# Weight chunks into one more place and in their filling order, and the last norm in halves ahead of the branch

## The chip, the cores and the metric

The kernel runs on one core of a Trainium2 chip. Its time is that of one launch in microseconds (us), the median of three runs. Matmuls run on TensorE (PE), element-wise work on VectorE (DVE), ScalarE (ACT) and GpSimd (POOL); SyncE (SP) issues nearly all DMAs, one after the other, from one queue. Where SP stands in a wait, every DMA written behind it waits too.

## The reference

Two blocks run over 256 tokens of width 1024. The first has two layers, each a mixer and 16 experts; the second has a token mixer and 32 experts, and a last norm. What matters here, cut down:

```python
def expert_choice_ffn(h, w_router, w_gate, w_up, w_down):   # 16 experts, 32 tokens each
    aff = softmax(h @ w_router)
    gate, idx = top_k(swapaxes(aff, 1, 2), cap)
    xe = h[bidx, idx]
    a = einsum('becd,edf->becf', xe, w_gate)
    u = einsum('becd,edf->becf', xe, w_up)
    ye = einsum('becf,efd->becd', silu(a) * u, w_down)
    return zeros_like(h).at[bidx, idx].add(gate[..., None] * ye)

def rmsnorm(x, g):
    return x * rsqrt(mean(x * x, axis=-1) + eps) * g
```

Every expert has three float32 matrices of its own, so nearly all bytes that the kernel reads are expert weights.

## The kernel before

**Stages.** `body` runs `mixer` and `experts` for layer 0 and for layer 1, then `token_mixer` and `moe`, then `final`. In each expert stage the weights come as chunks of 128 partitions x 2048 floats (1024 KB): `w_eg` and `w_ed` in the two layers, `w2eg` and `w2ed` in `moe`. PE reads a chunk at L810 (`w_eg`), L863 (`w_ed`), L1485 (`w2eg`) and L1524 (`w2ed`). In the mixers the weights are chunks too; there each is split into a high and a low part (L101, L102) and used at L121 to L123.

**Places.** `K.chunk` puts a chunk into a place of the tag that the ring names next: `K.use("WT")` means one in a W place, one in a T place, and so on in turn. There are 9 W places and 12 T places of 8 KB per partition. T places also hold whole tiles of the mixers (the names in `WHOLE`). Within a tag the places are taken in turn, so a chunk waits until the last reader of the tag's oldest place is done, even when a place of the other tag is free. At the start of an expert stage `ROOM` (or `ROOM2`) lists the tags of the chunks that are fetched ahead, while the mixer and the router still run; later chunks follow the ring set by the next `K.use`.

**Small places.** Tag P is four tiles of 2 KB per partition, taken in turn by softmax tiles, squares, `gs`, `yt`, `mt` and by `gb`, which a DMA fills in `ada_gate` (L632 and L633). Tag PT has four more, with `ht`, `sg` and others; `wh` and `wl` have three each, for the split weights. A DMA into such a tile stands on SP until the reader of the tile's former content is done.

**Order.** A scheduler fixes the order of instructions on each engine when the kernel is built. SP keeps the order in which the fetches are written (`issue_after` at L57).

**The end.** `moe_quad` does four experts together: the gate and up matmuls, then for each half of 512 columns the down matmuls (L1524), the scaling into `yt` (L1527), the split into `yd`, and the addition into `h` (L1533, L1535). Behind the last quad each engine loads a count (L1438) and branches (L1440): a second round, for tokens above the capacity, is skipped. Then `final` takes the squares of `h`, the inverse root (`rs`) and four products, and SP sends each out (L1546).

Of the kernel before, what the change touches and what calls it, by code (L numbers as in the profile page):

```python
# [2 lines left out]

# [1 line left out]

# [27 lines left out]
class Core:  # L33
    def __init__(self, ctx, tc, A):
        self.tc, self.nc, self.A = tc, tc.nc, A
        self.const = ctx.enter_context(tc.tile_pool(name="const", bufs=1))
        self.sb = ctx.enter_context(tc.tile_pool(name="sb", bufs=1))
        self.ps = ctx.enter_context(tc.tile_pool(name="ps", bufs=1, space=PSUM))
        self.flip = self.nsplit = self.nchunk = 0

        self.share = 4
        self.after = nullcontext
        self.idle, self.pre, self.sent = (), [], None
        self.use("W")

    def load(self, name, shape, dt=F):
# [116 lines left out]
    def rstd(self, src, n=D, dve=True, tag="P"):  # L163
        nc = self.nc
        ss = self.t([128, 2, 2], "ss", 2)
        for c in range(2):
            sl = slice(c * 512, (c + 1) * 512)
            for tt in range(2):
                sq = self.t([128, 512], "sq", SMALL[tag], tag=tag)
                if tt and dve:  # L170
# [546 lines left out]
def experts(K, h, l, mix, ada, prep, ahead=None):  # L717
# [74 lines left out]

    K.use(ROOM)
    ws = [K.chunk(A["w_eg"][l, i // KD, i % KD]) for i in range(len(ROOM))]
    K.use("WT" if ahead else FEW)
    hid, Ge = [], []
    gw = K.t([128, 4], "gw4")
    for e in range(NE):
# [19 lines left out]
        gs = K.t([128, 512], "gs", NP, tag="P")  # L818
# [628 lines left out]
def moe_round(K, h, hn, cmb, slot, gate=None):  # L1447
    nc, A = K.nc, K.A
    for q in range(NE2 // 8):
        oh = K.t([128, 2, 8, CAP2], "oh", 2, tag="oa", dt=FR)  # L1450
        for tt in range(2):
            nc.vector.tensor_tensor(oh[:, tt], slot[:, tt, 8 * q:8 * q + 8].unsqueeze(2).to_broadcast([128, 8, CAP2]),
                                    K.iota[:, 1:CAP2 + 1].unsqueeze(1).to_broadcast([128, 8, CAP2]), OP.is_equal)
        xT = K.t([128, KD, T], "xT", tag="hTa")
        for kb in range(KD):
            p = K.bank("sc")
            for n, (part_, tt) in enumerate(((0, 0), (0, 1), (1, 0), (1, 1))):
                nc.tensor.matmul(p[:, :T], lhsT=hn[part_][:, tt, kb * 128:(kb + 1) * 128],
                                 rhs=oh[:, tt].rearrange("p a b -> p (a b)"), start=(n == 0), stop=(n == 3))
            if kb % 2:  # L1460
                nc.scalar.activation(xT[:, kb, :], p[:, :T], AF.Identity, bias=K.B2[:, kb:kb + 1], scale=K.A2[:, kb:kb + 1])
            else:
                nc.vector.tensor_scalar(xT[:, kb, :], p[:, :T], K.A2[:, kb:kb + 1], K.B2[:, kb:kb + 1],
                                        op0=OP.mult, op1=OP.add)
        for i in (0, 4):
            moe_quad(K, h, xT, oh, cmb, 8 * q + i, i, gate)
            gate = None


def moe_quad(K, h, xT, oh, cmb, e, i, gate):  # L1470

    nc, A = K.nc, K.A
    hid = []
# [1 line left out]
    for pr in range(2):  # L1475
# [23 lines left out]
        if pr == 0:  # L1499
# [13 lines left out]
            for x in range(4):  # L1513
                nc.vector.tensor_copy(gw[32 * x:32 * x + 32, :], p[32 * x:32 * x + 32, T + x:T + x + 1])
    yd = K.t([128, 2, 1024], "yd", tag="V", dt=FR)
    for hf in range(2):
        sl = slice(hf * 512, (hf + 1) * 512)
        dn = K.bank("acc")
# [7 lines left out]
        y = K.t([128, 512], "yt", NP, tag="P")  # L1526
        nc.vector.scalar_tensor_tensor(y, dn, gw, K.gt[:, 1, sl], op0=OP.mult, op1=OP.mult)  # L1527
        hi, lo = yd[:, 0, sl], yd[:, 1, sl]
        K.split_to(hi, lo, y)
        for tt in range(2):  # L1530
            p = K.bank("sc")
            for n, part_ in enumerate((hi, lo)):
                nc.tensor.matmul(p, lhsT=Ge[:, tt * 128:(tt + 1) * 128], rhs=part_, start=(n == 0), stop=(n == 1))  # L1533
            hs = h[:, tt, sl]
            nc.vector.tensor_add(hs, p, hs)  # L1535


def final(K, h, out):
    nc = K.nc
    y = K.t([128, 2, D], "y", tag="hn")  # L1540
    rs = K.rstd(h)
    for tt in range(2):
        for c in range(2):
            sl = slice(c * 512, (c + 1) * 512)
            nc.vector.scalar_tensor_tensor(y[:, tt, sl], h[:, tt, sl], rs[:, tt:tt + 1], K.gf[:, sl], op0=OP.mult, op1=OP.mult)
            nc.sync.dma_start(out=out[:, tt, sl], in_=y[:, tt, sl])  # L1546
# [203 lines left out]
```

## Time and profile before

| what | value |
|---|---|
| median of 3 runs | 2229.97 us (2227.25 to 2230.5) |
| profiled execution | 2231.4 us |
| its span in the profile | 2229.6 us |
| mean granted TensorE clock | 0.915 |
| PE busy | 1803.5 us (81%) |
| DVE, ACT, POOL busy | 761.1, 600.3, 222.2 us |
| moved by DMA | 748.83 MB, mean 336 GB/s |
| chain that ended last | PE 40%, DMA 29%, issue 22%, DVE 6%, ACT 2% |

A single launch is profiled; 1.8 us of it lie outside the span. Times in rows count from the start of the span. The page cuts the span into 40 slices of 55.7 us.

### The profile page before, as it was taken

The numbers are of one execution on the slowest core, as the hardware profiler recorded it, in microseconds if no ns is written. First come the engines' busy times: TensorE is split into PE (matmuls) and PEld (weight loads), VectorE is DVE, ScalarE is ACT, GpSimd is POOL, SyncE is SP. The second block draws the span as 40 slices with busy tenths as digits, with TensorE's granted clock in tenths as the row PEclk, the third lists the DMA queues.
The fourth block names the chain that finished last, engine by engine and source line by source line (L and its number), as shares of the span: only waits on it lengthen the run. The fifth ranks groups of instructions, "written<-read, shape, count | busy, mean of one in ns | idle before, by whom it ended". The sixth has DMA issues, their size and how long they took to land.

```text
span 2229.6 us, 30070 instructions
## 1 busy us (share of the span) xinstructions
PE 1803.5 (81%) x12172; PEld 1017.9 (46%) x12172; DVE 761.1 (34%) x1696; ACT 600.3 (27%) x1191; POOL 222.2 (10%) x183
## 2 busy tenths in 40 slices
PE   8999996666699998987788666789999867676765
PEld 8888631110277776841234123368888412121211
DVE  5666510000045588532111111157557311111112
ACT  4666410000033357620125100055245200000000
POOL 2111200000011122300000000033134000000000
PEclk9999997777799999997799778889999999999998
DMA  8445779999999953569999999984223999999996
GB/s 342 149 146 207 313 311 420 422 421 421 421 418 419 414 210 151 216 264 399 420 420 420 421 419 420 418 337 156 76 70 149 418 420 421 420 421 421 421 421 284
DMA packets 108442, 748.83 MB, mean 336 GB/s; under 512 B 14120, under 2 KB 14537, under 8 KB 18697
## 3 DMA queue, kind: packets, MB, share of 16 engines
q1 hardware_dynamic: 107752, 745.79, 82.3%
q8 instruction: 98, 1.61, 0.3%
q10 hardware_dynamic: 544, 1.05, 0.1%
q14 instruction: 48, 0.39, 0.1%
HBM read 745.74 MB, written 1.05 MB: 335 GB/s over the span
## 4 chain that ended last, share of the span: by engine, by line
PE 40%; DMA 29%; issue 22%; DVE 6%; ACT 2%; POOL 0%; POOLq 0%; SPq 0%; ACTq 0%; DVEq 0%
DMA w<-in_w_eg 18%; DMA w<-in_w_ed 9%; PE mm L121 7%; PE mm L122 6%; PE mm L123 6%; PE acc L863 4%; PE mm L810 3%; PE sc L889 2%; DVE wl L102 1%; PE acc L518 1%; DMA w<-in_w2z 1%; PE acc L949 1%; PE acc L1228 1%; DMA cx<-in_ctx 1%; PE sc L122 1%
## 5 line engine op out<-in xcount | busy, mean ns | idle before, releaser
L810 PE MATMUL mm<-w,xT 128*32 128x512 f32 x2048 | 327.8, 743 | 116.6 <-DMA w<-in_w_eg 116.2
L101 ACT ACTIVATE wh<-w 128x512 fp32r<-128x512 f32 x384 | 239.9, 630 | 290.5 <-PE mm L122 218.0
L121 PE MATMUL mm<-hTa,wh 128*128 128x256 f32 x960 | 281.0, 294 | 5.6 <-DVE Ga L245 1.7
L123 PE MATMUL mm<-hTa,wl 128*128 128x256 f32 x960 | 274.2, 288 | 1.9 <-DVE wl L102 1.6
L122 PE MATMUL mm<-hTb,wh 128*128 128x256 f32 x960 | 272.5, 285 | 2.2 <-DVE hTb L113 1.6
L102 DVE TENSOR_TENSOR wl<-w,wh 128x512 fp32r<-128x512 f32 x286 | 220.1, 775 | 108.9 <-ACT wh L101 106.1
L1485 PE MATMUL mm<-w,xT 128*32 128x512 f32 x1024 | 176.9, 613 | 71.9 <-DMA w<-in_w2eg 71.4
L863 PE MATMUL acc<-w,hid 128*32 128x256 f32 x2048 | 184.7, 449 | 62.3 <-DMA w<-in_w_ed 62.3
L102 POOL TENSOR_TENSOR wl<-w,wh 128x512 fp32r<-128x512 f32 x98 | 129.0, 1317 | 901.9 <-ACT wh L101 803.9
L810 PEld LDWEIGHTS mm<-w,xT 128*32 128x32 f32 x2048 | 51.3, 120 | 329.6 <-DMA w<-in_w_eg 271.6
L121 PEld LDWEIGHTS mm<-hTa,wh 128*128 128x128 f32 x960 | 181.8, 190 | 28.4 <-issue 15.7
L123 PEld LDWEIGHTS mm<-hTa,wl 128*128 128x128 f32 x960 | 181.0, 190 | 10.6 <-issue 3.4
L122 PEld LDWEIGHTS mm<-hTb,wh 128*128 128x128 f32 x960 | 182.0, 190 | 6.2 <-issue 2.4
L863 PEld LDWEIGHTS acc<-w,hid 128*32 128x32 f32 x2048 | 80.5, 128 | 148.6 <-DMA w<-in_w_ed 83.1
L1524 PE MATMUL acc<-w,work 128*32 128x512 f32 x512 | 94.9, 640 | 32.9 <-DMA w<-in_w2ed 32.9
L1485 PEld LDWEIGHTS mm<-w,xT 128*32 128x32 f32 x1024 | 34.2, 110 | 189.1 <-DMA w<-in_w2eg 140.8
L178 POOL TENSOR_TENSOR rs<-rs,mhalf 128x2 f32<-128x2 f32 x9 | 6.8, 751 | 1008.4 <-DVE rs L177 1008.4
L826 DVE TENSOR_TENSOR hid<-tp,sg 128x256 f32<-128x256 f32 x32 | 13.6, 425 | 216.8 <-ACT sg L825 216.8
L113 DVE SCALAR_TENSOR_TENSOR yd<-acc,gw,yd 128x256 fp32r<-128x256 f32 x32 | 15.5, 483 | 181.2 <-ACT yd L112 181.2
L112 ACT ACTIVATE yd<-acc,gw 128x256 fp32r<-128x256 f32 x32 | 15.2, 475 | 220.0 <-PE acc L863 220.0
L91 DVE COPY gs<-mm 128x512 f32<-128x512 f32 x16 | 11.1, 692 | 181.5 <-PE mm L810 181.5
L825 ACT ACTIVATE sg<-tp 128x256 f32<-128x256 f32 x32 | 12.3, 384 | 218.3 <-PE tp L822 218.3
(468 smaller groups left out, 2471.8 us busy)
## 6 DMA issues: line engine op xcount, KB each, us to landing
w<-in_w_eg SPq DMA_DIRECT2D x256, 1024.0 KB, 19.8
w<-in_w_ed SPq DMA_DIRECT2D x128, 1024.0 KB, 18.5
w<-in_w2eg SPq DMA_DIRECT2D x128, 1024.0 KB, 19.8
w<-in_w2ed SPq DMA_DIRECT2D x63, 1024.0 KB, 19.8
w<-in_ada SPq DMA_DIRECT2D x24, 1024.0 KB, 11.7
w<-in_w_in SPq DMA_DIRECT2D x22, 1024.0 KB, 7.2
w<-in_wk SPq DMA_DIRECT2D x20, 1024.0 KB, 17.7
w<-in_w_b SPq DMA_DIRECT2D x8, 1024.0 KB, 6.0
```

The lines of the kernel that those rows point to most:

```text
L101: self.hi = nc.scalar.activation(hi, src, AF.Copy)
L102: (nc.gpsimd if n in self.idle or n % self.share == self.share - 1 else nc.vector).tensor_tensor(lo, src, hi.bitcast(F), OP.subtract)
L121: mm(out, lhsT=l[0], rhs=r[0], start=start, stop=False)
L122: mm(out, lhsT=l[0], rhs=r[1], start=False, stop=False)
L123: mm(out, lhsT=l[1], rhs=r[0], start=False, stop=stop)
L518: nc.tensor.matmul(po[half * 64:half * 64 + 64, :T], lhsT=V[:, kt, c:c + 64], rhs=PTs[half][:, kt * 256:(kt + 1) * 256], start=(kt == 0), ...
L810: nc.tensor.matmul(gu[32 * j:32 * j + 32, :], lhsT=xT[:, k, (e % 8) * CAP:(e % 8 + 1) * CAP], rhs=w[:, j * 512:(j + 1) * 512], start=(k == ...
L863: nc.tensor.matmul(dn[32 * x:32 * x + 32, :T], lhsT=hid[e // 8][:, e % 8, f, hh * 32:hh * 32 + 32], rhs=ws[x][:, fb * T:(fb + 1) * T], sta ...
L889: nc.tensor.matmul(p[:, :T], lhsT=hn[:, tt, kb * 128:(kb + 1) * 128], rhs=oh[:, tt].rearrange("p a b -> p (a b)"), start=(tt == 0), stop=( ...
L949: nc.tensor.matmul(p[:, :T], lhsT=w[:, o:o + 128], rhs=cT[:, k, :], start=(k == 0), stop=(k == KD - 1))
L1485: nc.tensor.matmul(gu[o:o + 32, :], lhsT=xT[:, k, y:y + CAP2], rhs=ws[x][:, (2 * kk + j) * 512:(2 * kk + j + 1) * 512], start=(k == 0), st ...
L1524: nc.tensor.matmul(dn[32 * x:32 * x + 32, :], lhsT=hid[x][:, c, :], rhs=wd[x][:, c * 512:(c + 1) * 512], start=(c == 0), stop=(c == 3), ti ...
```

## The change

1. The four P tiles of their own are gone. Tag P now takes a quarter of one T tile, held for a mixer; the room makes a 13th T place.
2. `ROOM` has 21 entries in place of 19 and `ROOM2` 18 in place of 16: one more T, and one "Q", a chunk that is fetched as four pieces of 512 columns into three `wh` tiles and a `wl` tile. The rings behind them (`AGAIN`, `AGAIN2`) repeat the order in which the places were filled.
3. `gb`, `gs` and `yt` move from P to PT.
4. In `moe_quad` the second half's down matmuls are written ahead of the first half's addition.
5. The last norm works in halves: the squares and the product with `gf` of half 0 stand in the last quad, the rest behind it and ahead of the branch; half 0 is scaled and sent by ACT, half 1 by DVE and SP. The same stands once more inside the branch.

```diff
     def chunk(self, src, parts=1):
         tag = next(self.ring)
+        if tag == "Q":
+            return self.quarters(src, ("wh", "wh", "wh", "wl"))
...
     def t(self, shape, name, bufs=1, tag=None, dt=F):
         tag = tag or name
+        if tag == "P":
+            if self.held is None:
+                self.held = self.sb.tile([128, PW], F, name="P4", tag="T", bufs=PLACES["T"]), cycle(range(0, PW, 512))
+            o = next(self.held[1])
+            return self.held[0][:, o:o + shape[1]]
...
-ROOM2 = "TWWTTTTWWTTTWWWW"
-ROOM, FEW = "TWWWWTTTTTTWWTTTWWW", "WWWWTWWWWWT"
-PLACES = {"W": 9, "T": 12}
+AGAIN, AGAIN2 = "WWWWTTTTTTWWTTTWWW", "WWTTTTWWTTTWWWW"
+ROOM2 = "TTWWTTTTWWTTQTWWWW"
+ROOM, FEW = "TTWWWWTTTTTTWWTTQTWWW", "WWWWTWWWWWT"
+PLACES = {"W": 9, "T": 13}
...
-    gb = K.t([128, 512], "gb", NP, tag="P")
+    gb = K.t([128, 512], "gb", NP, tag="PT")
...
-    K.use("WT" if ahead else FEW)
+    K.use(AGAIN if ahead else FEW, AGAIN)
...
     K.pre = [K.chunk(A["w2eg"][2 * i + x, c]) for i in range(2) for c in range(4) for x in range(2)]
-    K.use("WWTWT")
+    K.pre += [K.chunk(A["w2ed"][x, 0]) for x in range(len(ROOM2) - 16)]
+    K.use(AGAIN2)
...
-    moe_round(K, h, hs, cmb, slot, gate)
+    y = Final(K, h, out)
+    moe_round(K, h, hs, cmb, slot, gate, y.first)
+    y.second()
     n = nc.values_load(mi[0:1, 0:1], min_val=0, max_val=T)
...
+        if hf:
+            add(0)
+            if end and early:
+                early()
...
+    def first(self):
+        self.y = self.K.t([128, 2, D], "y", tag="hn")
+        self.squares(0)
+        for tt in range(2):
+            self.K.nc.vector.tensor_mul(self.y[:, tt, :512], self.h[:, tt, :512], self.K.gf[:, :512])
+
+    def second(self):
+        K, nc, y = self.K, self.K.nc, self.y
+        self.squares(1)
+        rs = K.inverse(self.ss)
+        for tt in range(2):
+            nc.scalar.activation(y[:, tt, :512], y[:, tt, :512], AF.Identity, scale=rs[:, tt:tt + 1])
+            nc.scalar.dma_start(out=self.out[:, tt, :512], in_=y[:, tt, :512])
+            nc.vector.scalar_tensor_tensor(y[:, tt, 512:], self.h[:, tt, 512:], rs[:, tt:tt + 1], K.gf[:, 512:], op0=OP.mult, op1=OP.mult)
+            nc.sync.dma_start(out=self.out[:, tt, 512:], in_=y[:, tt, 512:])
```

**SP at the start of the second block** (`token_mixer`): the last fetches of the gate's weights (`in_ada`), then `gb`, then the first weights of the mixer (`in_w2z`). In brackets stand the counters that an issue waits for: DMAHW0 to 7 count landings, the others are engines. Before:

```order
L58 DMA w<-in_ada 128x2048 [waits DMAHW5_49,PE_49]
L58 DMA w<-in_ada 128x2048 [waits DMAHW6_49,PE_49]
L58 DMA gb<-in_gtb 128x512 [waits DMAHW7_49,Activation_49]
L58 DMA w<-in_w2z 128x2048 [waits DMAHW0_49,PE_49]
L58 DMA w<-in_w2z 128x2048 [waits DMAHW1_49,PE_49]
```

And after the change:

```order
L58 DMA w<-in_ada 128x2048 [waits DMAHW3_49,PE_49]
L58 DMA w<-in_ada 128x2048 [waits DMAHW4_49,PE_49]
L58 DMA gb<-in_gtb 128x512 [waits DMAHW5_49,DVE_49,Activation_49]
L58 DMA w<-in_w2z 128x2048 [waits DMAHW6_49,PE_49]
L58 DMA w<-in_w2z 128x2048 [waits DMAHW7_49,PE_49]
```

The order of issues is the same; `gb` now waits for DVE as well. The PT tile that it takes held the fifth of the eight `ht` tiles of this block's start, whose last reader is the fifth `hTb` subtraction on DVE (L1052 before).

**SP at the start of the last expert stage** (`moe`): the gate's weights, `gb`, and the first chunks fetched ahead (`in_w2eg`). Before:

```order
L58 DMA w<-in_ada 128x2048 [waits DMAHW7_49,DVE_49,Pool_49]
L58 DMA gb<-in_gtb 128x512 [waits DMAHW0_49,Activation_49,Pool_49]
L58 DMA w<-in_w2eg 128x2048 [waits DMAHW1_49,PE_49]
L58 DMA w<-in_w2eg 128x2048 [waits DMAHW2_49]
L58 DMA w<-in_w2eg 128x2048 [waits DMAHW3_49]
```

And after the change:

```order
L58 DMA w<-in_ada 128x2048 [waits DMAHW5_49,DVE_49,Pool_49]
L58 DMA gb<-in_gtb 128x512 [waits DMAHW6_49]
L58 DMA w<-in_w2eg 128x2048 [waits DMAHW7_49,PE_49]
L58 DMA w<-in_w2eg 128x2048 [waits DMAHW0_49,PE_49]
L58 DMA w<-in_w2eg 128x2048 [waits DMAHW1_49,DVE_49,Pool_49]
```

Here `gb` no longer waits for ACT and POOL, only for a landing among its own counters; the chunks behind it have waits for engines of their own.

**PE and DVE at the end**, up to the branch: L1519 is the gate and up matmul (L1485 before), L1568 the down matmul (L1524), L1556 the addition's matmul (L1533). PE after the change:

```order
L1519 MATMUL mm<-w,xT 32x512 x32
L1526 MATMUL tp<-ident,work 128x128 x4
L1568 MATMUL acc<-w,work 32x512 x16
L1556 MATMUL sc<-yd,Ge 128x512 x4
L1568 MATMUL acc<-w,work 32x512 x16
L1556 MATMUL sc<-yd,Ge 128x512 x4
L1468 TENSOR_LOAD mi
```

DVE after the change:

```order
L1558 TENSOR_TENSOR h<-sc,h 128x512 x2
L1602 TENSOR_TENSOR y<-h,gf_13339 128x512
L1594 ISA sq,ss<-h 128x512
L1594 ISA ss 128x1
L1602 TENSOR_TENSOR y<-h,gf_13339 128x512
L1575 SCALAR_TENSOR_TENSOR yt<-acc,gw,gt 128x512
L126 TENSOR_TENSOR yd<-yt,yd 128x512
L1558 TENSOR_TENSOR h<-sc,h 128x512 x2
L1594 ISA sq,ss<-h 128x512
L1594 ISA ss 128x1
L197 TENSOR_TENSOR rs<-ss 128x2
L198 TENSOR_SCALAR rs<-rs 128x2
```

PE's order in the last quad is as it was before: 16 down matmuls, 4 of the addition, 16, 4. On DVE two products and a square of half 0 moved ahead of `yt` of half 1, and the rest of the norm ahead of the branch.

## Rows read from the trace of the kernel before

**Rows 1.** The page: GB/s moved in each of 40 slices of 55.7 us.

```profile
GB/s 342 149 146 207 313 311 420 422 421 421 421 418 419 414 210 151 216 264 399 420 420 420 421 419 420 418 337 156 76 70 149 418 420 421 420 421 421 421 421 284
```

**Rows 2.** Windows: busy us (instructions) of PE, PEld, DVE, ACT, POOL; PEclk, DMA share, GB/s.

```profile
280.00:290.00 10.00, 10.00 (x66) 4.57 (x65) 3.06 (x16) 0.95 (x2) 0.00 (x0) 1.00 0.28 107
...
610.00:790.00 180.00, 176.48 (x1636) 133.50 (x1628) 93.93 (x148) 60.42 (x107) 24.74 (x20) 0.99 1.01 415
```

**Rows 3.** Timeline of SP, layer 0's experts: start, us, instruction, count.

```profile
283.23 0.33 SPq L58 DMA_DIRECT2D w<-in_w_eg  x1
...
294.30 0.80 SPq L58 DMA_DIRECT2D w<-in_w_eg  x2
```

**Rows 4.** Timeline of PE at the third chunk read in layer 0's experts.

```profile
284.94 1.06 PE L810 MATMUL mm<-w,xT 128*32 128x512 f32 x8
```

**Rows 5.** DMA issues from 282 to 293 us: count, KB, us to landing.

```profile
w<-in_w_eg SPq DMA_DIRECT2D x1, 1024.0 KB, 4.7
```

**Rows 6.** Timeline of SP, layer 1's experts.

```profile
972.93 0.33 SPq L58 DMA_DIRECT2D w<-in_w_eg  x1
...
974.98 0.33 SPq L58 DMA_DIRECT2D w<-in_w_eg  x1
...
997.67 0.33 SPq L58 DMA_DIRECT2D w<-in_w_eg  x1
...
1002.71 0.33 SPq L58 DMA_DIRECT2D w<-in_w_eg  x1
```

**Rows 7.** Start of the last expert stage: SP's issues and wait, PE's last readers.

```profile
1687.27 0.33 SPq L58 DMA_DIRECT2D w<-in_ada  x1
...
1726.09 0.33 SPq L58 DMA_DIRECT2D gb<-in_gtb  x1
1726.51 15.33 SPq L58 DMA_DIRECT2D w<-in_w2eg  x13
...
SPq L58 <- POOL h L1317: 18.8, 1, 18.8
...
1710.89 0.28 PE L123 MATMUL mm<-yb,wl 128*128 128x256 f32 x1
...
1737.84 0.40 PE L123 MATMUL mm<-wh,mTb 128*128 128x512 f32 x1
```

**Rows 8.** Start of the second block: SP, DVE, PE, and two windows.

```profile
1460.78 0.33 SPq L58 DMA_DIRECT2D gb<-in_gtb  x1
...
1472.64 1.09 DVE L1052 TENSOR_TENSOR hTb<-ht,hTa 128x256 fp32r<-128x256 f32 x3
...
1468.44 0.58 PE L121 MATMUL mm<-hTa,wh 128*128 128x256 f32 x1
...
1470.00:1480.00 10.00, 7.96 (x60) 7.43 (x60) 7.03 (x17) 7.77 (x15) 2.97 (x3) 0.95 1.01 424
1480.00:1490.00 10.00, 10.00 (x87) 10.00 (x86) 3.47 (x5) 6.06 (x13) 6.48 (x6) 1.00 1.01 416
```

**Rows 9.** The end: timeline, the branch on PE, the landing of the outputs.

```profile
2213.10 0.75 DVE L1527 SCALAR_TENSOR_TENSOR yt<-acc,gw,gt 128x512 f32<-128x512 f32 x1 [2.60 <-PE acc L1524]
...
2215.84 1.29 DVE L1535 TENSOR_TENSOR h<-sc,h 128x512 f32<-128x512 f32 x2 [0.59 <-PE sc L1533]
2219.87 0.69 DVE L171 CUSTOM_DVE_ANT_0 sq<-h 128x512 f32<-128x512 f32 x1 [2.75 <-DVEq L1440]
2222.46 2.74 DVE L1545 SCALAR_TENSOR_TENSOR y<-h,rs,gf 128x512 f32<-128x512 f32 x4 [0.81 <-POOL rs L178]
...
L1440 PEldq COMPARE_BRANCH  x1: 3635/3635/3635, 2215.9 to 2215.9; - x1
...
out_y<-y SPq DMA_DIRECT2D x4, 256.0 KB, 3.2
```

**Rows 10.** The instructions that write tiles of tag P: count, ns min/median/max.

```profile
L417 ACT ACTIVATE P<-P,m x80: 492/506/725, 78.4 to 890.6; 128x256 f32<-128x256 f32 x64, 128x512 f32<-128x512 f32 x16
...
L506 DVE TENSOR_SCALAR P<-P,r x64: 341/349/1368, 134.4 to 894.3; 128x256 f32<-128x256 f32 x64
```

More of the change, by code (lines that the diff above doesn't have):

```diff
@@ L1 @@
 from contextlib import ExitStack, nullcontext
-from itertools import cycle, islice
+from itertools import chain, cycle, islice
 import numpy as np
@@ L42, in __init__ @@
         self.after = nullcontext
-        self.idle, self.pre, self.sent = (), [], None
+        self.idle, self.pre, self.sent, self.held = (), [], None, None
         self.use("W")
@@ L49, in load, with use @@
         return t
-    def use(self, places):
-        self.ring = cycle(places)
+    def use(self, places, first=""):
+        self.ring = chain(first, cycle(places))
     def fetch(self, out, src):
@@ L67, in chunk, with quarters @@
         return t
+    def quarters(self, src, tags):
+        ts = []
+        for i, tag in enumerate(tags):
+            ts.append(self.sb.tile([128, 512], F, name="w4", tag=tag, bufs=SMALL[tag]))
+            self.fetch(ts[-1], src[:, i * 512:(i + 1) * 512])
+        return Quarters(ts)
     def next_chunk(self, src, parts=1):
@@ L174, in rstd, with inverse @@
                     nc.scalar.activation(sq, src[:, tt, sl], AF.Square, accum_out=ss[:, tt, c:c + 1])
+        return self.inverse(ss, n)
+    def inverse(self, ss, n=D):
+        nc = self.nc
         r = self.t([128, 2], "rs", 2)
@@ L324, in mixer @@
     nc, A = K.nc, K.A
+    K.held = None
     if ahead:
@@ L724, in experts @@
         next(rt)
+    K.held = None
     q = K.logits
@@ L817, in experts @@
             hid.append(K.t([128, 8, 4, 64], "hid", tag=own[e // 8]))
[L818 removed]
+        gs = K.t([128, 512], "gs", NP, tag="PT")
         K.copy(gs, gu)
@@ L1033, in token_mixer @@
     nc, A, tc = K.nc, K.A, K.tc
+    K.held = None
     sc = K.t([128, 2, D], "sincos", tag="V")
@@ L1326, in token_mixer, with moe @@
         yield
-def moe(K, h, mix):
+def moe(K, h, mix, out):
     nc, A, tc = K.nc, K.A, K.tc
@@ L1344, in moe @@
         next(rt)
+    K.held = None
     q = K.logits
@@ L1444, in moe, with moe_round @@
             moe_round(K, h, hs, cmb, slot)
-def moe_round(K, h, hn, cmb, slot, gate=None):
+        K.sent = None
+        y = Final(K, h, out)
+        y.first()
+        y.second()
+def moe_round(K, h, hn, cmb, slot, gate=None, early=None):
     nc, A = K.nc, K.A
@@ L1465, in moe_round, with moe_quad @@
         for i in (0, 4):
-            moe_quad(K, h, xT, oh, cmb, 8 * q + i, i, gate)
+            moe_quad(K, h, xT, oh, cmb, 8 * q + i, i, gate, early)
             gate = None
-def moe_quad(K, h, xT, oh, cmb, e, i, gate):
+def moe_quad(K, h, xT, oh, cmb, e, i, gate, early):
     nc, A = K.nc, K.A
@@ L1515, in moe_quad, with add @@
     yd = K.t([128, 2, 1024], "yd", tag="V", dt=FR)
+    def add(hf):
+        sl = slice(hf * 512, (hf + 1) * 512)
+        for tt in range(2):
+            p = K.bank("sc")
+            for n, part_ in enumerate((yd[:, 0, sl], yd[:, 1, sl])):
+                nc.tensor.matmul(p, lhsT=Ge[:, tt * 128:(tt + 1) * 128], rhs=part_, start=(n == 0), stop=(n == 1))
+            hs = h[:, tt, sl]
+            nc.vector.tensor_add(hs, p, hs)
     for hf in range(2):
@@ L1525, in moe_quad @@
                                  start=(c == 0), stop=(c == 3), tile_position=(0, 32 * x))
-        y = K.t([128, 512], "yt", NP, tag="P")
-        nc.vector.scalar_tensor_tensor(y, dn, gw, K.gt[:, 1, sl], op0=OP.mult, op1=OP.mult)
-        hi, lo = yd[:, 0, sl], yd[:, 1, sl]
-        K.split_to(hi, lo, y)
-        for tt in range(2):
[L1531 to L1535, printed above, removed]
@@ L1538, in final @@
[L1538 to L1546, printed above, removed]
+        if hf:
+            add(0)
+            if end and early:
+                early()
+        y = K.t([128, 512], "yt", NP, tag="PT")
@@ new lines, in moe_quad, with __init__, squares @@
+        nc.vector.scalar_tensor_tensor(y, dn, gw, K.gt[:, 1, sl], op0=OP.mult, op1=OP.mult)
+        K.split_to(yd[:, 0, sl], yd[:, 1, sl], y)
+    add(1)
+class Final:
+    def __init__(self, K, h, out):
+        self.K, self.h, self.out = K, h, out
+        self.ss = K.t([128, 2, 2], "ss", 2)
+    def squares(self, c):
+        K, nc = self.K, self.K.nc
+        sl = slice(c * 512, (c + 1) * 512)
+        for tt in range(2):
+            sq = K.t([128, 512], "sq", NP, tag="PT")
+            h, ss = self.h[:, tt, sl], self.ss[:, tt, c:c + 1]
+            if tt:
+                nc.vector.tensor_tensor_reduce(sq, h, h, 1.0, 0.0, OP.mult, OP.add, ss)
+            else:
+                nc.scalar.activation(sq, h, AF.Square, accum_out=ss)
+    def first(self):
[7 more added lines that the diff above has]
+        rs = K.inverse(self.ss)
+        for tt in range(2):
+            nc.scalar.activation(y[:, tt, :512], y[:, tt, :512], AF.Identity, scale=rs[:, tt:tt + 1])
+            nc.scalar.dma_start(out=self.out[:, tt, :512], in_=y[:, tt, :512])
+            nc.vector.scalar_tensor_tensor(y[:, tt, 512:], self.h[:, tt, 512:], rs[:, tt:tt + 1], K.gf[:, 512:],
+                                           op0=OP.mult, op1=OP.mult)
+            nc.sync.dma_start(out=self.out[:, tt, 512:], in_=y[:, tt, 512:])
@@ L1576, in body @@
         dbg("h1", h)
-        moe(K, h, token_mixer(K, h))
+        moe(K, h, token_mixer(K, h), out)
         dbg("h3", h)
-        final(K, h, out)
 QORDER = [4 * (2 * (b // 4) + half) + b % 4 for b in range(8) for half in range(2)]
```

## The prediction

> **What bounds the kernel now.** I read the slices of the page first. About 420 GB/s are moved in three long stretches [rows 1], the expert stages: there a chunk of 1024 KB (1.049 MB) takes 1.049 MB / 421 GB/s = 2.49 us, and PE waits for it. Between the stretches the mixers are bound by computing. Where DMA is the bound to the end of a stretch, its length is bytes over rate, so time can be won only at its start: every chunk that lands earlier, before the queue is full for good, shifts all that follows by 2.49 us. I call that the lead. From 610 to 790 us both PE (176.5 of 180 us) and DMA are full [rows 2]; PE there works on what it got late, so a lead passes through.
>
> Next I read the starts of the stretches in the windows and on SP. In layer 0 the DMA share is 0.28 from 280 to 290 us, while PE is at 10.00 of 10 [rows 2]. SP issues one chunk at 283.23 and the next only at 294.30 [rows 3], though PE has finished a chunk every 2.05 us: two issues that wait for consecutive chunks, 972.93 and 974.98, show this pace [rows 6]. The ring asks for a T place there while W places stand free. A chunk issued into an idle queue lands after 4.7 us [rows 5], that is 2.2 us of start and 2.49 of transfer; so DMA is busy from 2.2 us after an issue on.
>
> **The change part by part.** All terms are made against the profiled execution (2231.4 us, span 2229.6); the median lies 1.4 us below it.
>
> *Layer 0's experts.* Two more chunks are fetched ahead (the 13th T place and the quarters). The first issue of the ring then waits for the third chunk read, whose matmuls end at 284.94 + 1.06 = 286.0 [rows 4]; I followed the tags of the new ring through, and its places come free in that order, about 2.05 us apart, which is faster than 2.49. So DMA is full from 286.0 + 2.2 = 288.2. Before, it was full from 294.30 + 2.2 = 296.5, with one chunk moved till then. Lead: 2 + (296.5 - 288.2) / 2.49 - 1 = 4.33 chunks = 10.8 us.
>
> *Layer 1's experts.* Before, seven chunks are issued from 972.93 to 997.67, and the queue fills from 1002.71 + 2.2 = 1004.9 [rows 6]. After, the ring starts with the release of 974.98, so DMA is full from 977.2: 2 + (1004.9 - 977.2) / 2.49 - 7 = 6.1 chunks, 15.3 us. Later in this stage the FEW ring follows, and by my walk through its places one issue is held near 1012 us for a chunk that PE reads late; I take 2 us off for it (a choice; 0 to 4). Lead: 13.2 us.
>
> *The last expert stage.* SP issues the last of `in_ada` at 1687.27 and `gb` only at 1726.09, because the P tile waits for POOL's addition at L1317; the w2eg chunks behind it start at 1726.51 [rows 7]. In PT the order shows `gb` waiting for neither ACT nor POOL, so it goes at about 1687.7. Of the chunks behind it the first finds its place free near 1695, the second when the matmul at 1710.89 ends, 1711.2 [rows 7], and seven more follow by 1728. DMA is full from 1711.2 + 2.2 = 1713.4, before from 1728.7: (1728.7 - 1713.4) / 2.49 + 1 = 7.1 chunks, 17.8 us. The next place comes free only with the matmul that ends at 1738.2 [rows 7], while the nine chunks are in by 1735.8: idle till 1740.2, 4.4 us given back. A second stall, where chunks behind the fetched-ahead ones wait for the first expert matmuls, I set at 2.5 us (0 to 5). Lead: 10.9 us. Nothing after 1730 is bound by PE for long, so this lead reaches the end.
>
> *The end.* Before, `h` is complete at 2215.84 + 1.29 = 2217.13; then DVE and ACT stand until PE's branch of 3.6 us (2215.9 to 2219.5) is over, squares of both halves start at 2219.87, and the products end at 2222.46 + 2.74 = 2225.20 [rows 9]. After, the squares and products of half 0 (0.69 + 0.77 + 0.69 = 2.15 us on DVE) lie in DVE's idle 2.60 us ahead of `yt` [rows 9]; without that cover they cost 2.15. Behind 2217.13 come one square (0.77), the chain from the last square to the first product (2221.18 to 2222.46, 1.28) and two products of 0.69 on DVE, with ACT beside it: 2220.55, 4.65 us earlier. SP now stands for the landing of the outputs (3.2 us) and only then branches. ACT, DVE and PE branch under that landing; for SP's branch I take 0.3 us, between nothing and PE's 3.6. Gain 4.3 us, range 1 to 4.7.
>
> The Trainium skill (Advanced Engine Details and Errata, Control Flow Timing) gives a compare-and-branch about 108 ns. The trace shows 3.6 us for PE's, and the measurement decides; by the page the branch held nothing and the gain here would be 3.5 us less, the sum 30.2.
>
> *Second half ahead of the first's addition.* PE's order in the last quad reads as before, 16, 4, 16, 4; other quads wait for DMA anyway. Nothing.
>
> *`gb` at the start of the second block.* This one costs. Before, it goes at 1460.78 and w2z behind it at once; PE starts on w2z at 1468.44 [rows 8]. Now `gb` waits for the fifth `hTb`, the first of three that start at 1472.64 [rows 8]: 1473.1 at the latest, about 1471.2 without the splits of w2z that lie between them before. Behind `gb` on SP stand all weights of the mixer. w2z is issued at 1471.6, lands with `gb` ahead of it near 1476.9, is split in 0.6 us, and PE starts at 1477.5, 9.1 us late. But before, PE did only 60 matmuls from 1470 to 1480, against 87 per 10 us afterwards [rows 8], because `hTb` came in piece by piece; after, all of it is there. 60 matmuls at 8.7 per us take 6.9 us, so they are done at 1484.4 in place of 1480: 4.4 us. With a slower first piece I take 5.5 us, range 3 to 9.1. PE is at 10.00 from 1480 on, so the delay goes through to the last stage.
>
> *P as quarters of one tile, `gs` and `yt` in PT.* No wait that I can name comes with it; DVE and ACT change their order a little in the mixers. Four operations of 0.75 us, as `yt` [rows 9], bound it from both sides: 0, range -3 to +3.
>
> Sum: 10.8 + 13.2 + 10.9 + 4.3 - 5.5 = 33.7 us. Profiled 2231.4 - 33.7 = 2197.7; the median, 1.4 lower, 2196.
>
> **The rivals.**
> (a) *Places only.* The order of places brings nothing, because the chunks that come free earlier only pile up ahead of a PE that is full (10.00 from 280 to 290 [rows 2]). Then two chunks per layer stage remain: 5.0 + 5.0 + 10.9 + 4.3 - 5.5 = 19.7 us, 2210. Against it: PE's 2.05 us per chunk is faster than 2.49, so it catches up within the stage.
> (b) *No loss at `gb`.* PE catches up after w2z, as DMA has weights waiting when it starts. 39.2 us, 2191.
> (c) *The quarters cost.* Four DMAs of 256 KB for one chunk. An output of 256 KB lands after 3.2 us [rows 9]; one after the other that is 12.8 us in place of 4.7, 8.1 us in each of three stages: 33.7 - 24.3 = 9.4, 2220. Against it: the four are issued back to back into a queue that is otherwise not full, and share it.
> The Trainium skill (DMA: Bandwidth & Descriptors, Rules for kernel authors) asks for at least 1 MiB per DMA, which speaks against the quarters. The outputs' 3.2 us for 256 KB beside 4.7 us for 1024 KB agree in direction; whether pieces that overlap pay it no row here shows.
> (d) *Slower.* The quarters of the held tile act as one place: each new P tile waits for the last read of its neighbours. L417 writes 80 softmax tiles, 506 ns each, and L506 scales 64 of them again, 349 ns [rows 10]. If each of the 80 waits for one such pair, 0.86 us, that is 68 us: 2231.4 + 68 - 33.7, median 2264. From 33.7 / 80 = 0.42 us per tile on it is slower. Against it: the order shows the softmax steps of neighbouring tiles still interleaved.
>
> **How the numbers follow.** Forecast 0.65; (a) 0.12; (b) 0.11; (c) 0.06; (d) 0.06. The forecast's own terms reach from about 2188 to 2206. The range 2187 to 2213 holds the forecast, (a) and (b) and leaves out (c) and (d) and the ends of the others. A difference under 0.2% (4.5 us) can't be told from none. Forecast, (a), (b) and (c) are faster by more than that, with 0.02 for a mixture that ends within it; (d) is slower where its wait per tile passes 0.42 us, 0.05 of its 0.06.
>
> **What would show it.** SP's issues in layer 0's experts at 286.0, 288, 290 and on, DMA full from about 288; in layer 1's from about 977. `gb` of the last stage at about 1688 (shifted by the leads so far) and w2eg right behind it. PE's first L121 of the second block some 9 us later against its layer's end, and the mixer 5 us longer. No idle of ACT and DVE for the branch, and outputs issued 3.5 us behind the last `h`. I am wrong if DMA falls idle again later in a stage by what it gained at the start, if the mixers of the first block grow by more than 3 us, or if a full second block hides a start that is 9 us late.

## The result and the profile after

The changed kernel takes 2201.83 us, median of 4 runs (2201.07 to 2202.3), beside 2229.28 us for the kernel before in the same runs: ratio 0.9877, 95% interval 0.986 to 0.9895. It is 27.5 us faster; 33.7 was forecast, and the time lies in the range. The profiled execution took 2202.3 us, its span is 2200.5 us, 29.1 less than before.

First the page of the changed kernel, GB/s in 40 slices (of 55.0 us now):

```profile
GB/s 342 142 151 229 321 348 420 421 421 421 420 418 420 416 214 154 234 339 396 420 420 420 420 420 420 418 286 170 77 58 264 353 421 420 421 420 420 421 421 298
```

Beside [rows 1] the three stretches at 420 are as high as they were; what rose are the slices ahead of them: 313, 311 became 321, 348; 216, 264 became 234, 339; 70, 149 became 58, 264. The time was won at the starts, not in the stretches.

To see where it was won I set the same instruction of both traces side by side (the n-th matmul of a line, counted from the start). Minus means earlier after the change:

| instruction | before | after | shift |
|---|---|---|---|
| first expert matmul of layer 0 (L810) | 280.04 | 279.37 | -0.7 |
| first w_ed matmul of layer 0 (L863) | 569.86 | 559.45 | -10.4 |
| first expert matmul of layer 1 | 969.74 | 958.47 | -11.3 |
| last expert matmul of layer 1 | 1451.72 | 1427.54 | -24.2 |
| 1345th L121, end of the token mixer | 1723.60 | 1705.61 | -18.0 |
| first expert matmul of the last stage (L1485) | 1756.83 | 1739.99 | -16.8 |
| last expert matmul (L1524) | 2212.39 | 2185.40 | -27.0 |
| end of the span | 2229.6 | 2200.5 | -29.1 |

So layer 0 gave 10.4 (forecast 10.8), layer 1 12.9 (13.2), the start of the second block cost 6.2 (5.5), the last expert stage gave 9.0 (10.9), and the end 2.1 (4.3). The rest, 0.9, lies between the two marks: 0.5 by the last w_ed matmul of layer 0 (781.07 to 770.18), 0.4 in the mixer of layer 1.

These are single executions, and they scatter. The kernels of experiments 1, 2, 7, 8 and 9 run the same instructions as the change up to the end of layer 1; their shifts are -6.3 to -11 at layer 0's first w_ed matmul, -9.8 to -12.9 at layer 1's first expert matmul and -23.7 to -26.6 at its end. So the layers agree with the forecast to within 2 or 3 us; that they agree to 0.4 is luck.

**The starts of the layers.** Windows of the kernel before, where DMA idled (columns as in [rows 2]; layer 0, then layer 1):

```profile
290.00:300.00 10.00, 10.00 (x65) 4.05 (x62) 1.79 (x4) 2.51 (x4) 0.00 (x0) 1.00 0.49 177
...
990.00:1000.00 10.00, 10.00 (x68) 4.42 (x66) 1.45 (x3) 1.37 (x3) 0.00 (x0) 1.00 0.32 117
```

Windows of the changed kernel, where layer 1 runs 11.3 us earlier, and SP's first issues behind the chunks fetched ahead:

```profile
280.00:290.00 10.00, 10.00 (x64) 4.96 (x60) 2.56 (x13) 0.95 (x2) 0.00 (x0) 1.00 0.36 130
290.00:300.00 10.00, 10.00 (x63) 4.08 (x62) 2.00 (x4) 2.51 (x4) 0.00 (x0) 1.00 0.95 382
...
980.00:990.00 10.00, 10.00 (x71) 3.90 (x70) 1.67 (x4) 0.95 (x2) 0.00 (x0) 1.00 1.01 420
```

```profile
285.39 0.33 SPq L58 DMA_DIRECT2D w<-in_w_eg  x1
287.45 0.33 SPq L58 DMA_DIRECT2D w<-in_w_eg  x1
...
963.71 0.33 SPq L58 DMA_DIRECT2D w<-in_w_eg  x1
965.77 0.33 SPq L58 DMA_DIRECT2D w<-in_w_eg  x1
```

In place of one issue and a gap of 11 us [rows 3] stand issues 2.06 us apart, from 285.39 (286.0 was forecast, less the 0.7 of the first row of the table); in layer 1 from 963.71, which is 974.98 less 11.3, as forecast. DMA is at 0.95 and 1.01 where it was at 0.49 and 0.32 before.

**The two gb tiles.** SP and PE of the changed kernel, at the start of the second block and of the last expert stage:

```profile
1446.30 0.33 SPq L58 DMA_DIRECT2D gb<-in_gtb  x1
...
1452.88 0.58 PE L137 MATMUL mm<-hTa,wh 128*128 128x256 f32 x1 [7.61 <-ACT wh L117]
...
1669.76 0.44 SPq L58 DMA_DIRECT2D gb<-in_gtb  x1
1677.15 0.33 SPq L58 DMA_DIRECT2D w<-in_w2eg  x1
...
1693.21 0.80 SPq L58 DMA_DIRECT2D w<-in_w2eg  x2
...
1720.01 1.28 SPq L58 DMA_DIRECT2D w<-in_w2eg  x3
```

On the old time scale (24.2 us later) the first `gb` goes at 1470.5 where it went at 1460.78 [rows 8], and PE stands 7.61 us until w2z is there and split. The second goes at 1669.76; in the last stage (18.0 us later on the old scale) the chunks follow at 1695.1, 1711.2 and 1738.0, the three times that the prediction took from [rows 7].

**The end.** Timeline of the changed kernel from the last addition into `h`:

```profile
2188.76 1.29 DVE L1558 TENSOR_TENSOR h<-sc,h 128x512 f32<-128x512 f32 x2 [0.59 <-PE sc L1556]
...
2190.08 0.69 DVE L1594 CUSTOM_DVE_ANT_0 sq<-h 128x512 f32<-128x512 f32 x1
...
2192.06 1.33 ACT L1609 ACTIVATE y<-y,rs 128x512 f32<-128x512 f32 x2 [1.79 <-POOL rs L199]
2192.06 1.41 DVE L1611 SCALAR_TENSOR_TENSOR y<-h,rs,gf 128x512 f32<-128x512 f32 x2 [0.81 <-POOL rs L199]
2192.81 2.08 ACTq L1610 DMA_DIRECT2D out_y<-y  x2
2192.84 2.04 SPq L1613 DMA_DIRECT2D out_y<-y  x2
```

And what stands on the line of the branch (count, ns min/median/max, first and last start); SP's eight EVENT_SEMAPHOREs are its waits for the landings:

```profile
L1470 SPq EVENT_SEMAPHORE  x8: 17/17/17, 2198.6 to 2199.1; - x8
L1470 PEldq COMPARE_BRANCH  x1: 3572/3572/3572, 2188.8 to 2188.8; - x1
...
L1470 SPq COMPARE_BRANCH  x1: 50/50/50, 2194.9 to 2194.9; - x1
```

DVE and ACT no longer stand for the branch: DVE's square starts 0.03 us behind the last `h`, and PE's 3.6 us of branch lie beside it. From the last `h` (2190.05) to the last product (2193.47) it takes 3.42 us, before 8.07: 4.65 won, to the hundredth what was forecast.

Behind the products some of this is lost again. Each output raises its counter 16 times in the trace; by these counts the last one has landed at 2197.95, 4.5 us behind the last product, where it was 3.3 before (2228.46). The bytes moved, in 40 slices of 0.3 us from 2188 to 2200, agree: those of the outputs end before 2197.6 (the single 55s and the 27 are loads of instructions):

```profile
GB/s 0 0 0 0 0 0 55 0 0 0 0 0 0 0 0 0 55 0 14 355 362 355 335 205 164 382 403 389 362 191 48 14 0 0 0 0 0 27 0 0
```

SP's first wait passes only at 2198.59, 0.64 us behind that landing and 3.6 us behind SP's branch; in the kernel before it passed 0.02 us behind the landing.

### The profile page after: what moved, and what is told of

Read it like the earlier page. It is cut to its first block, busy times and chain, and to the rows that moved or that the text cites. A ratio compares the mean times of both kernels' runs of the same rounds, so it can differ in the third digit from the quotient of the medians.

```text
span 2200.5 us, 30093 instructions
## 1 busy us (share of the span) xinstructions
PE 1794.2 (82%) x12172; PEld 1014.4 (46%) x12172; DVE 761.8 (35%) x1696; ACT 601.0 (27%) x1193; POOL 220.7 (10%) x183
## 4 chain that ended last, share of the span: by engine, by line
DMA 49%; PE 42%; DVE 6%; issue 1%; ACT 1%; POOL 0%; SPq 0%; POOLq 0%; DVEq 0%; ACTq 0%
DMA w<-in_w_eg 21%; DMA w<-in_w2eg 12%; DMA w<-in_w_ed 9%; PE mm L137 7%; PE mm L139 6%; DMA w<-in_w2ed 6%; PE mm L138 6%; PE acc L888 4%; PE mm L835 2%; PE sc L914 2%; DVE wl L118 1%; DMA w<-in_w2z 1%; PE acc L542 1%; PE acc L1568 1%; PE acc L1254 1%
## 5 line engine op out<-in xcount | busy, mean ns | idle before, releaser
L888 PE MATMUL acc<-w,hid 128*32 128x256 f32 x2048 | 180.1, 435 | 67.4 <-DMA w<-in_w_ed 67.3
L1519 PE MATMUL mm<-w,xT 128*32 128x512 f32 x1024 | 181.7, 661 | 56.2 <-DMA w<-in_w2eg 55.9
L139 PEld LDWEIGHTS mm<-hTa,wl 128*128 128x128 f32 x960 | 181.4, 190 | 11.2 <-issue 3.9
L1568 PE MATMUL acc<-w,work 128*32 128x512 f32 x512 | 96.1, 639 | 31.8 <-DMA w<-in_w2ed 31.8
L1519 PEld LDWEIGHTS mm<-w,xT 128*32 128x32 f32 x1024 | 35.1, 114 | 173.5 <-DMA w<-in_w2eg 119.2
L107 DVE COPY gs<-mm 128x512 f32<-128x512 f32 x16 | 11.1, 692 | 161.5 <-PE mm L835 161.5
## 6 DMA issues: line engine op xcount, KB each, us to landing
w<-in_ada SPq DMA_DIRECT2D x24, 1024.0 KB, 12.2
w<-in_wk SPq DMA_DIRECT2D x20, 1024.0 KB, 19.9
```

The costliest lines, as they stand in the source:

```text
L139: mm(out, lhsT=l[1], rhs=r[0], start=False, stop=stop)
L888: nc.tensor.matmul(dn[32 * x:32 * x + 32, :T], lhsT=hid[e // 8][:, e % 8, f, hh * 32:hh * 32 + 32], rhs=ws[x][:, fb * T:(fb + 1) * T], sta ...
L1519: nc.tensor.matmul(gu[o:o + 32, :], lhsT=xT[:, k, y:y + CAP2], rhs=ws[x][:, (2 * kk + j) * 512:(2 * kk + j + 1) * 512], start=(k == 0), st ...
```

## The experiments

Each edit is made to the changed kernel unless said otherwise. The kernel before took 2229.5 to 2230.3 us beside them.

**1. The first gb on the P tile again.**

```diff
-    gb = K.t([128, 512], "gb", NP, tag="PT")
+    gb = K.t([128, 512], "gb", NP, tag="PT" if g else "P")
```

> The changed kernel with one edit: the first of the two gb tiles (start of the second block) is a quarter of the held P tile again, not a PT tile. Theory: that gb then waits for ACT's squares alone, w2z follows on SP some 10 us earlier, and PE starts on it some 6 us earlier against the end of layer 1; the leads before and after stay. The second block's start keeps the 24 us won by then instead of falling to 18: about 6 us faster than the changed kernel, 2196. Rival: PE catches up on w2z anyway, and the 6 us have another cause (the order of DVE's work in the mixer): 2202, the same as the changed kernel.

Measured: 2193.12 us (2191.71 to 2194.51), ratio 0.9835 (0.9818 to 0.9851), 8.7 us faster than the change. SP and PE of this kernel at the start of the second block:

```profile
1434.25 0.33 SPq L58 DMA_DIRECT2D P<-in_gtb  x1
1434.67 2.47 SPq L58 DMA_DIRECT2D w<-in_w2z  x4
...
1441.59 0.58 PE L137 MATMUL mm<-hTa,wh 128*128 128x256 f32 x1
```

PE's wait of 7.61 us is gone; the shift is -26.6 at the end of layer 1, -26.8 at the end of the token mixer, and -26.8 at the first matmul of the last stage. The 6.2 us came from `gb`. The profiled executions differ by more, 10.6 us: 2.4 of that lie in the layers, which run the same instructions in both kernels (scatter), and 1.6 in the last stage (see below). This kernel beats both.

**2. The second gb waits again.** Tag P for `g` = 1, and the held tile isn't given up ahead of it:

```diff
-    gb = K.t([128, 512], "gb", NP, tag="PT")
+    gb = K.t([128, 512], "gb", NP, tag="P" if g else "PT")
...
-    K.held = None
     q = K.logits
```

> The changed kernel with one edit: the second gb (start of the last expert stage) is a quarter of the P tile that the token mixer holds, so that it waits for POOL's addition again, as before the change. Theory: SP stands there and the w2eg chunks start about 39 us later; the lead of this stage (8.9 us in the changed kernel) goes, but for what two more chunks fetched ahead may keep: 2209 to 2212. Rival: those chunks only land earlier and stand idle, since the lead comes from the places: 2202, as changed.

Measured: 2211.46 us (2210.37 to 2213.02), 9.6 us slower than the change. The waits of SP's queue in this kernel, from 1665 to 1712 us:

```profile
SPq L58 <- ACT mTa L125: 19.6, 1, 19.6
SPq L58 <- POOL h L1343: 18.8, 1, 18.8
```

This is the wait of [rows 7] with its 18.8 us, and the lead of the last stage is gone with it: -17.0 at the end of the mixer, -16.5 at the last expert matmul.

**3. The old rings with the new places.**

```diff
-    K.use(AGAIN if ahead else FEW, AGAIN)
+    K.use("WT" if ahead else FEW)
...
-    K.use(AGAIN2)
+    K.use("WWTWT")
```

> The changed kernel with the old rings behind the chunks fetched ahead (WT, FEW, WWTWT); the 13th T place, the quarters and the two more chunks stay. Theory: the order of places gave more than half of the leads. In layer 0 the second issue behind the chunks fetched ahead comes at about 294 instead of 288: 5.8 us lost; in layer 1 the ring holds SP from about 983 to 997 (on the old time scale): about 10 us lost; in the last stage nothing. 2218. Rival (a) of the prediction: the places alone did it, 2202, as changed.

Measured: 2218.55 us (2216.89 to 2220.51), ratio 0.995 (0.9933 to 0.9966). Windows of this kernel, columns as in [rows 2]:

```profile
290.00:300.00 10.00, 10.00 (x63) 4.52 (x56) 2.18 (x5) 2.51 (x4) 0.00 (x0) 1.00 0.64 235
...
980.00:990.00 10.00, 10.00 (x68) 5.04 (x70) 1.45 (x3) 1.42 (x3) 0.00 (x0) 1.00 0.16 46
```

DMA idles again where the ring asks for the place of a chunk not yet read, 0.16 against 1.01 from 980 to 990. The leads are 4.7 us at layer 0's first w_ed matmul, 9.3 at the first expert matmul of layer 1 and 11.3 at its end, where the change has 10.4, 11.3 and 24.2. Most of the loss lies in layer 1. Rival (a) falls.

**4. The rings alone, in the kernel before.** 12 T places, P, gb and the end stay; only AGAIN and AGAIN2 follow the chunks fetched ahead.

```diff
-    K.use("WT" if ahead else FEW)
+    K.use(AGAIN if ahead else FEW, AGAIN)
...
-    K.use("WWTWT")
+    K.use(AGAIN2)
```

> The kernel before with one edit: the rings behind the chunks fetched ahead repeat the order in which the places were filled (AGAIN, AGAIN2); 12 T places, 19 and 16 chunks ahead, P, gb and the end as before. Theory: in layer 0 the second issue of the ring comes at about 286 instead of 294, in layer 1 SP no longer stands from 983 to 997: leads of about 8 and 11 us; nothing in the last stage, where gb holds SP, and nothing at the end: 2230 - 19 = 2211. Rival (a), places only: nothing, 2230.

Measured: 2214.05 us, three of the four runs within 2210.94 to 2214.14 and one at 2220.5; ratio 0.9939 (0.9922 to 0.9955). In the profiled execution (2210.94) the shift is -17.8 at the end of layer 1, -20.0 at the end of the token mixer and -19.9 at the last expert matmul: 18 or so from the two layers, nothing from the last stage, as expected, and 2.2 between the end of layer 1 and that of the token mixer, which was not forecast. The median is 3 us above what was expected, and the runs lie too far apart to say more.

**5. No quarters.**

```diff
-ROOM2 = "TTWWTTTTWWTTQTWWWW"
-ROOM, FEW = "TTWWWWTTTTTTWWTTQTWWW", "WWWWTWWWWWT"
+ROOM2 = "TTWWTTTTWWTTTWWWW"
+ROOM, FEW = "TTWWWWTTTTTTWWTTTWWW", "WWWWTWWWWWT"
```

> The changed kernel without the Q entries: 20 chunks and 17 chunks are fetched ahead in place of 21 and 18, and no chunk comes in quarters. Theory: one chunk of lead less in each of the three stages while the first issue behind them stays where it is (it waits for the same read), 3 x 2.5 = 7.5 us: 2209. Rival (c): the quarters cost more than they bring, and without them it is the same or faster: 2195 to 2202.

Measured: 2210.08 us (2205.64 to 2212.45), 8.2 us slower than the change; in the trace 6.5 at the last expert matmul (-20.5 for -27.0). The quarters pay about what was expected in all, and rival (c) falls. In this trace the 6.5 are 4.3 up to layer 1, nothing in layer 1 and 2.4 in the last stage; one chunk in each of the three is not shown.

The quarters are not free. Four us of the last stage in the changed kernel, in which its quarters move, and below them the same stretch in the kernel without quarters:

```profile
1726.00:1730.00 4.00, 3.48 (x28) 1.46 (x30) 3.17 (x7) 2.25 (x3) 0.00 (x0) 0.99 0.88 287
...
1728.00:1732.00 4.00, 3.48 (x17) 1.99 (x20) 2.01 (x5) 3.94 (x6) 0.41 (x1) 0.76 1.02 430
```

At 287 GB/s for 430 some 1.3 us of transfer are lost there. The Trainium skill (DMA: Bandwidth & Descriptors, Rules for kernel authors) asks for 1 MiB or more per DMA; the trace agrees in direction, but a chunk that is there early is worth more than that.

**6. P as tiles of its own, 12 T places.** The block for tag P goes out of `t`, and one T from the front of each list:

```diff
-        if tag == "P":
...
-ROOM2 = "TTWWTTTTWWTTQTWWWW"
-ROOM, FEW = "TTWWWWTTTTTTWWTTQTWWW", "WWWWTWWWWWT"
-PLACES = {"W": 9, "T": 13}
+ROOM2 = "TWWTTTTWWTTQTWWWW"
+ROOM, FEW = "TWWWWTTTTTTWWTTQTWWW", "WWWWTWWWWWT"
+PLACES = {"W": 9, "T": 12}
```

> The changed kernel with P as four tiles of its own again and 12 T places, and so one T entry less among the chunks fetched ahead (20 and 17); the quarters and the rings stay. Theory: in the layers the 13th place brings nearly nothing, since with one chunk fewer ahead the ring's first issue waits for the read before (about 283.2 in place of 286.0 in layer 0, 972.9 in place of 975.0 in layer 1, on the old time scale), so the queue fills that much earlier: 0 to 1 us in each; in the last stage, where places are short, 2.5 us: 2202 to 2206. The prediction's count of two chunks: 7.5 us, 2209. Rival (d): quarters of one tile cost in the mixers; then the stretch up to layer 0's experts and between the layers is shorter here by more than 1 us.

Measured: 2208.16 us, but from 2205.18 to 2213.0 over four runs, so the total does not tell 2206 from 2209. The trace (of the fastest run) does better: the lead is 12.2 us at layer 1's first expert matmul and 25.8 at its end, where the change has 11.3 and 24.2; 19.3 becomes 23.9 over the last stage, where the change goes from 18.0 to 27.0. In the layers the 13th place brings nothing that stands out of the scatter: its first issue behind the chunks fetched ahead comes one read earlier (281.99 for 285.39, 960.74 for 963.71), as expected. In the last stage the place is worth 4.4 us, more than the 2.5 expected. Between layer 0's last w_ed matmul and layer 1's first expert matmul this kernel takes 187.2 us and the changed one 188.3; but five kernels that hold P in one tile take 187.3 to 188.7 there, so nothing is left that speaks for rival (d).

**7. The old end.** The norm whole and behind the branch, four outputs from SP:

```diff
-    moe_round(K, h, hs, cmb, slot, gate, y.first)
-    y.second()
+    moe_round(K, h, hs, cmb, slot, gate)
...
+    final(K, h, out)
```

> The changed kernel with the last norm as it was, whole and behind the branch, its four outputs from SP. Theory: the end (from the last addition into h to the end of the span) takes 12.5 us again instead of 10.5: about 2 us slower than the changed kernel, 2204, because the landing of the outputs takes 5.1 us behind the last issue where it took 3.2. Rival: the prediction's 4.3 us: 2206.

Measured: 2205.12 us (2202.64 to 2205.33), 3.3 us slower than the change. In its profile the last `h` is done at 2190.99 and the span ends at 2203.2, 12.2 us; 10.45 in the change. By the profiles the new end is worth 1.7 to 2 us; the medians allow a little more. This stretch scatters too: 10.15 to 11.2 us in seven kernels with the new end and 12.0 in that of experiment 3, 12.0 to 12.5 in the three with the old one.

**8. All outputs from SP.**

```diff
-            nc.scalar.dma_start(out=self.out[:, tt, :512], in_=y[:, tt, :512])
+            nc.sync.dma_start(out=self.out[:, tt, :512], in_=y[:, tt, :512])
```

> The changed kernel with one edit: all four outputs are issued by SP, none by ACT. In the changed kernel the first two issues (ACT and SP, 0.03 us apart) take 0.39 and 0.35 us, the second two 1.47 and 1.38, and the last landing comes 5.1 us behind the last issue, where it was 3.2 before the change. Theory: issuing from two engines at the same moment makes this longer; from SP alone each issue takes 0.33 to 0.35 again, the fourth goes at about 2194.3, and the end comes about 1 us earlier. Rival: it comes from the products being done at once, so that four outputs are in flight together: the landing stays at 4 to 5 us, and the end is the same or up to 1 us later. The total, 2201 to 2203, can't tell them apart; the rows at the end can.

Measured: 2204.14 us (2199.99 to 2205.15), not to be told from the change. The end of this kernel:

```profile
2195.04 0.35 SPq L1610 DMA_DIRECT2D out_y<-y  x1
2195.48 1.54 SPq L1613 DMA_DIRECT2D out_y<-y  x1
2197.11 0.38 SPq L1610 DMA_DIRECT2D out_y<-y  x1
2197.59 0.39 SPq L1613 DMA_DIRECT2D out_y<-y  x1
```

And its waits behind the branch (count, ns, first and last start):

```profile
L1470 SPq EVENT_SEMAPHORE  x8: 17/17/17, 2201.4 to 2202.0; - x8
```

My theory falls: one issue takes 1.54 us with a single engine as well, here the second of four. The landing times that I expected from in experiments 7 and 8 were too late, though: I had taken the moment at which SP's first wait passes for the last landing. By the counts it is 2197.95 in the change and 2200.79 here. From the first issue to the last landing it takes 5.1 us in the change (from 2192.81), 5.8 here (from 2195.04), 5.2 before (2223.24 to 2228.46). The Trainium skill (DMA: Bandwidth & Descriptors, Issuing engines are not separate DMA queues) says that a second issuing engine saves only issue time; the runs agree: the four issues take 2.1 us on two engines and 2.9 on SP, and from the last `h` to the end of the span it is 10.45 and 11.1.

**9. The first gb and all outputs from SP together.**

> The two edits together: the first gb on the P tile, and all outputs from SP. From the first alone 2193.1; with the theory on the outputs 1 us less, 2192; with its rival the same or up to 1 us more. Faster than both kernels either way.

Measured: 2192.84 us, median of 5 (2192.21 to 2194.78), ratio 0.9838 (0.9824 to 0.9852): the same as experiment 1 alone. From the last `h` to the end of the span it takes 11.1 us here and 10.15 in experiment 1, so the outputs are better left on two engines, if that is more than scatter.

## Why the prediction was right, and where it was off

**Layers 0 and 1: right, in mechanism and size.** The issue times, the 2.06 us between them and, within the scatter, the leads came as worked out. Experiments 3 and 4 show from both sides that the order of places is most of it: without it 11.3 us remain of the 24.2 at the end of layer 1, and alone it gives 17.8. The two add up to more than 24.2, and layer 0 is where they overlap: in the middle of its w_ed stretch the lead is 7.8 us without the new order, 7.5 with it alone and 11.6 with all, though the prediction simply added 5.0 for the chunks and 5.8 for the order. In layer 1 the order is nearly all of it. Experiments 5 and 6 correct the count "two more chunks": a chunk more ahead in the ring's own places lets the first issue behind it wait for one read more, so the two cancel within the scatter, while the quarters, which lie in places that the ring doesn't use, are worth 6.5 to 8 us over the kernel.

**The first gb: right, sized low.** 6.2 us for 5.5 (5.9 to 6.8 in five other kernels with this `gb`, 9.4 in a sixth). PE's start was 8.7 us late (1452.88 + 24.2 = 1477.1, for 1468.44), 9.1 forecast. Two windows of the changed kernel show what probably slowed the catch-up:

```profile
1440.00:1450.00 10.00, 3.50 (x16) 2.27 (x16) 6.09 (x18) 6.14 (x9) 0.00 (x0) 0.64 0.26 89
1450.00:1460.00 10.00, 7.12 (x45) 6.90 (x46) 2.59 (x4) 4.40 (x7) 1.29 (x1) 0.68 1.01 426
```

The granted clock is 0.64 and 0.68, partly at 1.2 GHz in place of 2.4, after PE had stood; before, it was 0.95 from 1470 to 1480 [rows 8]. Experiment 1 gives back the 6.2 us. Rival (b), no loss here, falls.

**The last expert stage: right in mechanism, 1.9 us too much.** The term mis-sized is the second stall, which I set at 2.5 us. Counted in bytes moved, at 421 GB/s and against the end of the token mixer, the changed kernel is 18.0 us of transfer ahead at the peak (forecast 17.8), 13.4 behind the first stall (4.6 lost, forecast 4.4) and 9.1 in the end: 4.3 lost behind the first stall, of which some 1 while the quarters move. PE of the kernel before, at the router:

```profile
1752.33 0.41 PE L1394 MATMUL tp<-rt,cb 128*128 128x64 f32 x2 [2.76 <-issue]
```

PE of the changed kernel, from the router to the first expert:

```profile
1735.33 0.41 PE L1421 MATMUL tp<-rt,cb 128*128 128x64 f32 x2 [3.79 <-issue]
...
1739.99 1.94 PE L1519 MATMUL mm<-w,xT 128*32 128x512 f32 x8
1741.86 1.22 PE L1492 MATMUL sc<-oh,ht 128*128 128x256 f32 x4
```

Between the gate's matmuls and L1421 PE stands 3.79 us, before 2.76: five small DVE operations of the router's weights, 0.2 us each, now stand ahead of the one that PE waits for. At 1752.33 before and 1735.33 after the shift is only -17.0. The first expert matmuls then run at a lower clock (granted 0.69 from 1740 to 1745) and take 1.94 us; the second group starts at 1743.01, before at 1758.86, so by then 2.2 of the 18.0 us are lost, and the places come free that much later. In experiments 1 and 9 the five operations stand behind it, as before; PE stands 2.77 and 2.76 us there, 2.4 and 2.2 us are lost behind the first stall, and the last stage gives 10.6 and 11.2 us. In experiments 3, 7 and 8 PE stands 3.78 or 3.79 us, as in the change, and it gives 8.6, 8.4 and 9.4. So the step behind the missing 1.9 us is the one that put the changed order of DVE's operations at 0: the prediction had it in mind for the mixers only. An edit of this order alone was not run.

**The end: the last step failed.** The products were done 4.65 us earlier, as worked out. The step "SP now stands for the landing of the outputs (3.2 us) and only then branches", with 0.3 us for that branch, was wrong in both parts. First, 3.2 us was the landing of an output that had been issued some 0.7 us behind the one before it; from the first issue to the last landing it takes 5.1 us after the change and 5.2 before. So what counts is the first issue: 6.11 us behind the last `h` before (2217.13 to 2223.24), 2.76 after, 3.35 won. Second, SP branches ahead of its waits, at 2194.93, and the 0.05 us of that instruction are not its cost. The first wait passes 0.6 us later behind the last landing than it did before, and 0.8 are lost because SP now goes through its list of eight landings twice, at the branch and at the end. That leaves the 2.0 measured.

In the eight kernels with this end SP's first wait passes 3.1 to 5.0 us behind SP's branch; in seven of them all outputs had landed 0.2 to 0.8 us earlier, so the landing wasn't what held it last, and it passes 1.0 to 1.4 us behind the end of a load of 8 KB of instructions. PE's branch takes 3.4 to 4.0 us in the same kernels. That SP, like PE, waits there for instructions to be loaded is what these times suggest; no run tried it.

**The second half ahead of the first's addition: not tried.** The order of the matmuls on PE in the last quad is as it was, which is why nothing was forecast; no run had this part alone.

**The rivals.** (a), (b) and (c) fell in experiments 3, 1 and 5, though in the last stage the quarters do cost some 1.3 us of transfer. (d) fell in experiment 6.

## What to carry to other kernels

Where transfers bound a long stretch, read its first 20 us: a queue that asks for its places in another order than they come free stands behind a place still in use while others lie empty, and most of that is lost for good. A small DMA in the same queue is a gate for all that is written behind it; before its tile is moved to another pool, look up whose reader it will then wait for, at each of its uses (here one use gained 9 us and the other lost 6). Before work on one engine changes, look at what the scheduler does with the order of the others: five small operations moved ahead went with a loss of 2 us here. For the last outputs count from the first issue to the last landing, not the landing of one, and don't take the record of a branch for its cost: look when the next instruction of that engine comes.

## What was not expected of the hardware

Some of the four last issues take 0.8 to 1.9 us in place of 0.35 when the outputs are ready together: the second on each engine in the change (1.47 and 1.38), the second or the third when SP issues all (1.54 and 1.88). From the first issue to the last landing it takes 4.8 to 6.1 us in all versions, with the long issues or without.

The long issues go with loads of instructions. In each of the seven kernels that have one it ends 0.3 to 0.7 us behind the end of a 16 KB load (in the change from 2193.08 to 2194.19; the two issues end at 2194.9). In the kernel before and in experiments 4 and 7 no such load runs beside the issues, and all four are short; in experiment 5 it starts just as the last two are being made, and they are short too. Whether the load holds the issue was not tried.
